# Gate blocks moved from the prompt's attention to the sample's attention, and a compression bias made once per cache, in a hybrid decoder step

## The chip, the cores and the metric

The kernel runs on one core of one Trainium2 chip. The metric is the time of one execution in microseconds (us) of device time; lower is better. Times of before are three runs, and one further execution was recorded by the profiler.

## What is computed

One layer of a hybrid trunk on 1024 prompt positions and 8 x 4 sample positions (1056 columns together, 1024 features). Two mixers run on the same normalised input: a gated MLP (mixer A), and sparse attention with a compressed, a selected and a window branch (mixer B). Their outputs pass through sigmoid gates and an output projection, and an MLP follows. In the reference's words:

```
x = x + (sigmoid(g_a) * (o_a @ w_branch[:A]) + sigmoid(g_b) * (o_b @ w_branch[A:])) @ w_out
h = rms_norm(x, g_norm2)
return x + square(relu(h @ w_up)) @ w_down
```

The compression that feeds the compressed branch is, per cache (keys, values):

```
bias = pe.reshape(-1) @ w1
return gelu(first[:, :-1] + second[:, 1:] + bias) @ w2
```

It is done once for the prompt's own rows and once for each of the sample's 8 caches of 2048 positions. `pe` and `w1` are the same for both, so `bias` is the same as well. For the sample, the selected branch reads 13 of 32 key blocks; the kernel reads all of them and masks.

## The kernel before, in words

Weight matrices are cut into 128-column blocks, 102 in all. Of these, block numbers 0 to 15 of a set that the code calls FM_MG give the merge gates (tanh of half the sum, stored to `th_d`), and 16 to 19 give mixer A's `u` (gelu, multiplied with the stored `s_d`, stored to `o_d`). "Gate block" stands for any of these 20 below. A gate block is worked in three column chunks of 352 columns; one chunk is 24 matmuls into one bank `G`, since each 32-bit operand is split into a high and a low part and three products are summed over 8 k-tiles. Weight blocks pass through a class `Weights`: a load (tile `wraw`), a high part on ACT and a low part by a subtraction on GpSimd (tile `whl`), one block ahead.

The stages, in program order:

1. Projections of keys, values, queries, and mixer A's `v`.
2. The prompt's attention: 32 pairs (8 query blocks of 128, 4 head pairs). For pair u, `a_steps` makes logits in bank `S` (three buffers), maxima on DVE, exponentials on ACT, a scale on GpSimd; `c_steps` transposes the probabilities (bank `PT`, `T`), splits them into two parts (tile `PH`, ACT then DVE) and multiplies with V in bank `O` (`PV`); `E` stores the result (tile `o_o`). Query block 7 has 27 key blocks to a pair.
3. The compression of the sample's caches (`c_weights`, 16 units, bank `F`); it is emitted after the attention, and is scheduled into it.
4. The sample's attention: two groups G of four sequences, each with five chunks c (four of selected keys, one of the window): ten chunks in all. One chunk is 2 MB in one of two `ring` buffers (NRB = 2): 16 page loads on SP, of 128 KB, or four loads of 512 KB for the window. A chunk is logits (`s_logits`, four matmuls j, one for each sequence, each needs its own four page loads), a masked maximum on DVE, an exponential on ACT, four transposes, and `values` (16 matmuls into `O`), which is the last reader of the ring buffer. Then `fin_group`.
5. What is left of the gate blocks, then the branch projection (`half_block`: tiles `OA`, from mixer B's output, and `OU`, from mixer A's), output projection and MLP to the end.

Tiles are assigned to engines by hand, but the order within an engine is set by a scheduler that follows data dependences and priority; earlier code has the higher priority. SP's order is kept as written in stages 3 and 4. So a gate block that is written late (line 1240 in before) may stand much earlier, where the scheduler saw room for it. It needs only the input `X`, a weight tile and bank `G`. The weight tiles of `W0` (pool `wst0`) are free from the start of the prompt's attention; those of `W1` (pool `wst`) lie where the attention's keys and values were (pool `kvp`) and so wait for its end.

NF0 says how many gate blocks belong to `W0` and NF1 is a second such number; before has 17 and 0. `OA` lies where the sample's ring was, and `OU` where `X` was, so neither can be filled before the sample's last `values` and the last gate block, respectively. Both are read back from `o_d` through four `ol` buffers.

Of the kernel before, what the change touches and what calls it, by code (L numbers as in the profile page):

```python
# [15 lines left out]
TB = 352  # L16
# [8 lines left out]
FM_KC, FM_VC, FM_MG, FM_U, FM_BR, FM_OUT, FM_MLP = 0, 1, 2, 18, 22, 30, 38  # L25
RAWA = 2
NRB = 2
DB = ("G", 1), ("F", 1), ("O", 1), ("PT", 2), ("PT", 2), ("S", 3), ("S", 3), ("S", 3)
NF0, NF1 = 17, 0
SB, FB = 3, 1  # L30
XRB = 4
QB = ("G", 1), ("F", 1)
# [13 lines left out]
def build(tc, a):  # L46
# [12 lines left out]
    def add(out, x, y):  # L59
        return tt(out, x, y, OP.add)  # L60
# [82 lines left out]
    knt = const("knt", [128, 2, 32])  # L143
    vn = const("vn", [32, 2, 128])
    expo = const("expo", [128, 16])
    onesf = const("onesf", [128, 2])

    X = big.tile([128, 2, 8, NT], F32R, name="big1")
    KT = kvp.tile([128, 4, NP], F32R, name="KT")
# [10 lines left out]
    def powcol(out, in_, n):  # L160
        POOL.tensor_tensor(out, in_, expo[:, 0:n], op=OP.pow)

    POOL.memset(onesf, 1.0)
    DVE.memset(f(ones), 1.0)
    cp(expo, f(ones)[:, 0:16], scale=-0.5)

# [259 lines left out]
        SP.dma_start(pe, a["pe" + "kv"[which]])  # L426
        return w1, pe, comp_w2(which, pl)

    def comp_bias(w1, pe, ps, pl):
        for o in range(8):  # L430
            mm(ps, w1[:, o], pe[:, o], o == 0, o == 7)
        tb = small([64, 2], "tb", 2, p=pl)
        cp(tb[:, 0:1], ps[64:128, 1:2])
        add(tb[:, 1:2], ps[0:64, 0:1], tb[:, 0:1])
        return tb[:, 1:2]

    def comp_hidden(ps, nch, bias, pl):

# [43 lines left out]
    def compress_prompt(which):  # L482
        w1, pe, w2 = comp_consts(which, pc)
        c2 = craw[which]
        pb = bank("F", 1) if which == 0 else bank("PT", 2)
        for o in range(8):
            mm(pb[:, 0:128], w1[:, o], c2[:, :, o], o == 0, o == 7)
        pbb = bank("G", 1) if which == 0 else bank("PT", 2)
        bias = comp_bias(w1, pe, pbb[:, 0:2], pc)
        g = comp_hidden(pb[:, 0:128].rearrange("p (k c) -> p k c", k=2), 64, bias, pc)  # L490
        DVE.tensor_copy(g[:, 64:128], g[:, 0:64])
        pb2 = bank("G", 1) if which == 0 else bank("O", 1)
        comp_out(pb2[:, 0:128], g, w2)
        if which == 0:
            z = comp_knorm(pb2[:, 0:128], pc, gkc, 2)
            ks = small([128, 2, 2, 64], "ckx", 1, F32R, p=pc)
            z3 = z.rearrange("p (h d) -> p h d", d=64)
            DVE.tensor_copy(ks[:, :, 0], z3)
            sub(ks[:, :, 1], z3, f(ks[:, :, 0]))
            pt = bank("F", 1)  # L500
            for kv in range(2):
                PE.transpose(pt[:, kv * 128:(kv + 1) * 128], f(ks[:, kv].rearrange("p a d -> p (a d)")), ident)
            cp(KTC, pt[:, 0:256].rearrange("p (k c) -> p k c", k=2)[:, :, 0:64])
        else:
            z3 = pb2[:, 0:128].rearrange("p (h d) -> p h d", d=64)
            POOL.memset(f(V2C), 0.0)
            for h in range(2):
                r = slice(64 * h, 64 * h + 64)
                cp(V2C[r, h, :, 0], z3[r])
                sub(V2C[r, h, :, 1], z3[r], f(V2C[r, h, :, 0]))  # L510
# [440 lines left out]
    def c_weights(which):  # L951
        w1r = pa.tile([128, 8, 128], F32, name="w1r", tag="hl", bufs=HIB)
        ACT.dma_start(w1r, a["w1" + "kv"[which]])
        w1 = pa.tile([128, 2, 8, 128], F32R, name="w1s", bufs=1)
        split(w1[:, 0], w1[:, 1], w1r)
        pe = small([128, 8, 2], "pes", 1, p=pa)
        ACT.dma_start(pe, a["pe" + "kv"[which]])
        w2 = comp_w2(which, pa)
        pb = bank("F", FB, psS)
        return w1, comp_bias(w1r, pe, pb[:, 0:2], pa), w2  # L960

    cl = Ahead([lambda w=w, b=b: c_load(w, b) for w in range(2) for b in range(8)], RAWA)
    ctxm = tc.manual_schedule(engines={mybir.EngineType.SP})
# [44 lines left out]
    def fillers(W, blocks, tag):  # L1008
        n = 0
        for b in blocks:  # L1010
# [12 lines left out]
                    evac(b, c, cs, ps)  # L1023
            W.ahead()

    def gate_evac3(b, c, cs, ps):
        zt = wst0.tile([128, TB], F32, name="zt", bufs=2) if b < NF0 else fp.tile([128, TB], F32, name="yt", bufs=2)
        mul(zt, ps[:, 0:TB], rep[:, cs])
        ACT.activation(zt, zt, AF.Tanh, scale=0.5)
        (ACT if b < 8 else POOL).dma_start(th_d[b, :, cs], zt)  # L1030
# [12 lines left out]
        POOL.dma_start(o_d[b - 16, :, cs], y)  # L1043

    W0 = Weights(wst0, 1, range(FM_MG, FM_MG + NF0))
    ps3 = pool("ps3")
    p3 = pool("p3")
    regs.clear()
# [99 lines left out]
        DVE.tensor_reduce(nm[:, 5:7], pn, axis=AX.X, op=OP.max, negate=True)  # L1148
        news.append((pn, nm))
    hp.__exit__(None, None, None)  # L1150
    fillers(W1, range(NF0, NF0 + NF1), lambda i: "S")

    def values(oc, c, blocks):

# [37 lines left out]
    for G in range(2):  # L1192
        pn, nm = news[G]
        sm = small([128, 8], "s_sm", 2, p=p3)
        oc = p3.tile([128, 6, 128], F32, name="oc", bufs=2)
        pt = bank("PT", 2, psS)
        PE.transpose(pt[:, 0:128], pcs[G], ident)
        ph = p3.tile([128, 5, 128], F32, name="s_ph", bufs=2)
        cp(ph[:, 0], pt[:, 0:128])
        values(oc, 5, [(ph[:, 0], vct[:, 4 * G:4 * G + 4])])  # L1200
        for c in range(5):
            br = c // 4
            kv = kvl()
            S = bank("S", SB, psS)
            s_logits(S, qp, G, lambda j: kv[:, :, j, 0:128])
            P = p3.tile([128, 512], F32, name="s_P", bufs=3)
            if c < 4:
                DVE.tensor_tensor_reduce(P.rearrange("p (b k) -> p b k", k=64), S.rearrange("p (b k) -> p b k", k=64),
                                         smask[:, G, c * 8:(c + 1) * 8, None].to_broadcast([128, 8, 64]),
                                         scale=-1.0, scalar=3e38, op0=OP.add, op1=OP.min, accum_out=nm[:, c:c + 1])  # L1210
            else:
                add(S[:, 0:4], S[:, 0:4], mwc)
                DVE.tensor_reduce(nm[:, c:c + 1], S, axis=AX.X, op=OP.max, negate=True)
            if c % 4 == 0:
                tt(nm[:, c:c + 1], nm[:, c:c + 1], nm[:, 5 + br:6 + br], OP.min)
                ACT.activation(pn[:, br], pn[:, br], AF.Exp, bias=nm[:, c:c + 1], accum_out=sm[:, 5 + br:6 + br])
            ACT.activation(P, P if c < 4 else S, AF.Exp, bias=nm[:, c:c + 1], scale=-1.0 if c < 4 else 1.0,
                           accum_out=sm[:, c:c + 1])
            ph = p3.tile([128, 5, 128], F32, name="s_ph", bufs=2)
            if c % 4 == 0:  # L1220
                pt = bank("F", FB, psS)
                PE.transpose(pt[0:32, 0:128], pn[:, br], ident)
                cp(ph[0:32, 4], pt[0:32, 0:128])
            pt = bank("PT", 2, psS).rearrange("p (a t) -> p a t", t=128)
            for e in range(4):
                PE.transpose(pt[:, e], P[:, e * 128:(e + 1) * 128], ident)
            cp(ph[:, 0:4], pt)
            blocks = [(ph[:, e], kv[:, e, :, 128:256]) for e in range(4)]
            if c % 4 == 0:
                blocks.append((ph[0:32, 4], vn[:, br]))  # L1230
            values(oc, c, blocks)
            if c == 1 and done:
                fin_group(*done)
        done = G, nm, sm, oc
# [2 lines left out]
    p3.release()  # L1237
    ps3.release()

    fillers(W0, range(NF0), lambda i: "G")  # L1240
    fillers(W1, range(NF0 + NF1, 20), lambda i: "GF"[i % 2])
    fp.release()
    wst0.release()

# [293 lines left out]
```

## Time and profile of before

| | us |
|---|---|
| median of 3 runs | 1848.17 |
| lowest and highest | 1847.6, 1854.99 |
| the profiled execution, device time | 1848.68 |
| its span, first to last instruction | 1846.9 |
| TensorE busy | 1761.8 (95%) |
| DVE, ACT, GpSimd busy | 949.0, 703.1, 414.0 |
| mean granted TensorE clock | 0.982 |

Busy time of an engine is the time in which it had at least one instruction in work; matmuls overlap, so a listed duration is longer than the distance between starts. The granted clock is 1.00 at TensorE's upper level (2.4 GHz) and 0.50 at its lower one (1.2 GHz); a value in between is a stretch with both. All positions are in us from the span's start.

### The profile page before, as it was taken

To read this page: it belongs to the slowest core of one execution; us is meant where nothing else is said; L and a number is where in the kernel's file an instruction comes from. 1 tells how busy PE (TensorE), PEld (TensorE's weight loads), DVE (VectorE), ACT (ScalarE), POOL (GpSimd) and SP (SyncE) were. 2 spreads that over 40 slices of the span, in tenths; PEclk is the share of its full clock that TensorE was granted. 3 is DMA by queue.
4 is the path that set the end of the run, shared out by engine and by line. 5 is a ranking of instruction groups with operands and counts; after the bars stand their busy time and mean duration, and the time that the engine had idled before them with its cause. 6 is when DMAs were issued, how large, how long until landed. Compare 5 with 4: busy or idle time off the path is not lost.

```text
span 1846.9 us, 30397 instructions
## 1 busy us (share of the span) xinstructions
PE 1761.8 (95%) x11127; PEld 1659.8 (90%) x11127; DVE 949.0 (51%) x2373; ACT 703.1 (38%) x1683; POOL 414.0 (22%) x604
## 2 busy tenths in 40 slices
PE   8999989999899999876999999999999999999999
PEld 6877889999899998523999999999999999999999
DVE  7637878777767777211765445333333333333332
ACT  5534577767667765211422332200330033003300
POOL 3103456555556655200200220000000000000000
PEclk9999989999999999987999999999999999999999
DMA  5332454333323313664553221111111111111121
GB/s 198 95 95 64 142 151 124 93 95 89 98 68 98 96 63 121 205 189 149 183 161 121 92 77 46 46 46 46 46 46 46 46 47 46 46 46 46 45 78 64
DMA packets 157992, 168.75 MB, mean 91 GB/s; under 512 B 52113, under 2 KB 132626, under 8 KB 157842
## 3 DMA queue, kind: packets, MB, share of 16 engines
q1 hardware_dynamic: 140194, 135.77, 23.9%
q0 software_dynamic: 6464, 20.19, 3.3%
q10 hardware_dynamic: 11184, 10.83, 1.8%
q8 instruction: 88, 1.44, 0.3%
q14 instruction: 62, 0.51, 0.1%
HBM read 136.56 MB, written 29.13 MB: 90 GB/s over the span
## 4 chain that ended last, share of the span: by engine, by line
PE 80%; DVE 5%; SPq 5%; DMA 3%; ACT 3%; issue 2%; POOL 1%; ACTq 0%; DVEq 0%; POOLq 0%; another core or an unknown queue 0%
PE S L73 26%; PE G L73 16%; PE PT L73 14%; PE F L73 10%; PE O L73 10%; SPq L932 3%; PE PT L844 3%; SPq L924 2%; DMA ol<-o_d 1%; ACT P L783 1%; PE PT L699 1%; DVE S L774 1%; DMA xr<-xT 0%; DVE PH L57 0%; ACT PH L54 0%
## 5 line engine op out<-in xcount | busy, mean ns | idle before, releaser
L54 ACT ACTIVATE whl<-wraw 128x1024 fp32r<-128x1024 f32 x100 | 106.1, 1061 | 411.2 <-PE S L73 144.2
L73 PE MATMUL G<-big,whl 128*128 128x352 f32 x1344 | 255.2, 333 | 2.5 <-ACT whl L54 1.5
L73 PEld LDWEIGHTS G<-big,whl 128*128 128x128 f32 x1344 | 220.6, 193 | 13.4 <-issue 5.0
L73 PE MATMUL S<-U,whl 128*128 128x352 f32 x864 | 201.6, 324 | 0.0
L73 PE MATMUL S<-H,whl 128*128 128x352 f32 x840 | 190.4, 324 | 0.0
L73 PE MATMUL PT<-U,whl 128*128 128x352 f32 x576 | 154.9, 324 | 0.0
L73 PEld LDWEIGHTS S<-U,whl 128*128 128x128 f32 x864 | 150.0, 188 | 0.0
L798 POOL TENSOR_SCALAR P<-P,rs 128x128 f32<-128x128 f32 (+4 forms) x272 | 132.8, 504 | 63.7 <-DVE rs L57 43.0
L73 PEld LDWEIGHTS S<-H,whl 128*128 128x128 f32 x840 | 144.9, 188 | 0.0
L73 PE MATMUL PT<-H,whl 128*128 128x352 f32 x528 | 143.2, 324 | 0.0
L783 ACT ACTIVATE P<-S,nm 128x512 f32<-128x512 f32 (+3 forms) x208 | 109.0, 532 | 44.1 <-DVE nm L57 32.9
L73 PE MATMUL S<-wt,big 128*128 128x512 f32 x408 | 104.1, 402 | 10.0 <-ACT wt L54 6.5
L57 DVE TENSOR_TENSOR PH<-PT,PH 128x512 fp32r<-128x512 f32 (+2 forms) x160 | 98.2, 618 | 29.6 <-ACT PH L54 28.1
L118 DVE TENSOR_TENSOR whl<-wraw,whl 128x1024 fp32r<-128x1024 f32 x80 | 97.7, 1222 | 14.6 <-ACT whl L54 14.6
L73 PEld LDWEIGHTS PT<-U,whl 128*128 128x128 f32 x576 | 103.3, 188 | 0.0
L73 PE MATMUL F<-H,whl 128*128 128x352 f32 x312 | 101.1, 324 | 0.0
L73 PE MATMUL O<-PH,V 128*128 128x256 f32 x528 | 92.1, 296 | 9.4 <-DVE PH L57 9.0
L73 PEld LDWEIGHTS S<-wt,big 128*128 128x128 f32 x408 | 76.1, 191 | 27.2 <-ACT wt L54 6.5
L54 ACT ACTIVATE PH<-PT 128x512 fp32r<-128x512 f32 (+2 forms) x160 | 86.1, 545 | 36.2 <-PE PT L844 35.3
L73 PE MATMUL O<-H,whl 128*128 128x352 f32 x312 | 99.0, 324 | 0.0
L73 PE MATMUL S<-KT,QT 128*128 128x128 f32 (+3 forms) x416 | 95.5, 340 | 2.9 <-ACT P L783 2.1
L73 PE MATMUL G<-H,whl 128*128 128x352 f32 x312 | 97.5, 324 | 0.5 <-DVE r L1373 0.5
(376 smaller groups left out, 3821.2 us busy)
## 6 DMA issues: line engine op xcount, KB each, us to landing
wraw<-wfm SPq DMA_DIRECT2D x80, 512.0 KB, 3.2
ring<-cs SPq DMA_DIRECT2D x128, 128.0 KB, 2.4
wraw<-wfm POOLq DMA_DIRECT2D x20, 512.0 KB, 3.9
tg<-th_d SPq DMA_DIRECT2D x48, 176.0 KB, 2.9
qdl<-qd_d SPq DMA_DIRECT2D x64, 128.0 KB, 2.5
raw<-cck SPq DMA_DIRECT2D x128, 64.0 KB, 1.8
raw<-ccv SPq DMA_DIRECT2D x128, 64.0 KB, 1.8
wtr<-wtok SPq DMA_DIRECT2D x24, 256.0 KB, 2.7
```

Source lines behind the costliest of these rows:

```text
L54: return ACT.activation(out, in_, AF.Copy, scale=scale)
L57: return DVE.tensor_tensor(out, x, y, op=op)
L73: return PE.matmul(out, l, r, start=start, stop=stop, skip_group_check=skip)
L118: (POOL if i < FM_BR else DVE).tensor_tensor(t[:, 1], raw, f(t[:, 0]), op=OP.subtract)
L699: PE.transpose(pt[:, j], src[:, j], ident)
L774: DVE.tensor_tensor_reduce(S, S, m, scale=-1.0, scalar=3e38, op0=OP.add, op1=OP.min, accum_out=dst)
L783: ACT.activation(Ps[c][:, lo:hi], Ss[c][:, lo:hi], AF.Exp, bias=nm[:, 0, k:k + 1], scale=todo[h, br, i], accum_out=sm[:, i, k:k + 1])
L798: POOL.tensor_scalar(P, P, rs[:, 1, k:k + 1], 1.0, op0=OP.mult, op1=OP.mult)
L844: PE.transpose(pt[:, j], Ps[c][:, j * 128:(j + 1) * 128], ident)
L924: _, vals = nc.values_load_multi_w_load_instructions(ptab[0:1, i0:i0 + 16], engines=[mybir.EngineType.SP], min_val=0, max_val=159, skip_ru ...
L932: SP.dma_start(dst, src)
```

## The change

NF0 becomes 12 and NF1 becomes 2. `W0`'s 12 blocks are still written so that the scheduler may place them anywhere from the start of the prompt's attention on; they are now written ahead of the sample's attention instead of behind it. The other eight (block numbers 12 to 19, `W1`) go through a generator, `fill`, which yields after each column chunk; the sample's loop takes two of them (NF1) right behind each chunk's logits, so 20 of the 24 column chunks stand in the loop, and the remaining four are taken behind it. All use bank `G`; before, the last three blocks alternated between `G` and `F`. The compression's bias is kept in a constant tile `cbias` when the prompt's compression makes it, and `c_weights` no longer loads `pe` or makes it again.

```diff
-NF0, NF1 = 17, 0
+NF0, NF1 = 12, 2
...
-    def comp_bias(w1, pe, ps, pl):
+    def comp_bias(which, w1, pe, ps, pl):
...
-        add(tb[:, 1:2], ps[0:64, 0:1], tb[:, 0:1])
-        return tb[:, 1:2]
+        add(cbias[:, which:which + 1], ps[0:64, 0:1], tb[:, 0:1])
+        return cbias[:, which:which + 1]
...
-        pe = small([128, 8, 2], "pes", 1, p=pa)
-        ACT.dma_start(pe, a["pe" + "kv"[which]])
         w2 = comp_w2(which, pa)
-        pb = bank("F", FB, psS)
-        return w1, comp_bias(w1r, pe, pb[:, 0:2], pa), w2
+        return w1, cbias[:, which:which + 1], w2
...
+    def fill(W, blocks, tag):
+        for b in blocks:
+            w = W.get(FM_MG + b)
+            for c in range(3):
+                cs = slice(c * TB, (c + 1) * TB)
+                ps = bank(tag, 1, psS)
+                for k in range(8):
+                    mm(ps[:, 0:TB], w[:, 0, k], X[:, 0, k, cs], k == 0, False)
+                    mm(ps[:, 0:TB], w[:, 0, k], X[:, 1, k, cs], False, False)
+                    mm(ps[:, 0:TB], w[:, 1, k], X[:, 0, k, cs], False, k == 7)
+                with tc.high_priority():
+                    (gate_evac3 if b < 16 else u_evac)(b, c, cs, ps)
+                if c == 2:
+                    W.ahead()
+                yield
...
     W0 = Weights(wst0, 1, range(FM_MG, FM_MG + NF0))
+    fillers(W0, range(NF0), lambda i: "G")
...
-    fillers(W1, range(NF0, NF0 + NF1), lambda i: "S")
+    f1 = fill(W1, range(NF0, 20), "G")
...
             s_logits(S, qp, G, lambda j: kv[:, :, j, 0:128])
+            for _ in range(NF1):
+                next(f1, None)
...
-    fillers(W0, range(NF0), lambda i: "G")
-    fillers(W1, range(NF0 + NF1, 20), lambda i: "GF"[i % 2])
+    for _ in f1:
+        pass
```

Three places show how the order on TensorE moves. The first is the end of the prompt's attention (`O_67..<-PH` is the last pair's `PV`, `V2C` its last operand; `G_` with `whl` is a gate chunk). Before:

```order
L73 MATMUL G_11856<-big1_77,whl_11851 128x352 x22
L73 MATMUL O_6768<-PH_6825,V2_80 128x256 x2
L73 MATMUL O_6768<-PH_6825,V2C_81 128x256 x2
L73 MATMUL G_11885<-big1_77,whl_11851 128x352 x24
L73 MATMUL G_11914<-big1_77,whl_11851 128x352 x24
```

Now:

```order
L843 MATMUL PT_6820<-ident_68,P_6710 128x128 x3
L73 MATMUL O_6767<-PH_6813,V2_80 128x256 x4
L1211 MATMUL PT_9911<-ident_68,pcs_9795 128x128
L73 MATMUL O_6767<-PH_6824,V2_80 128x256 x2
L73 MATMUL O_6767<-PH_6824,V2C_81 128x256 x2
L73 MATMUL G_10229<-big1_77,whl_10226 128x352 x2
L73 MATMUL F_9896<-knt_73,qp_9866 32x32 x8
```

Before, gate chunks run through to the end of the attention, and 1104 of the 1440 gate matmuls stand ahead of its last matmul. Now 864 do (all of `W0`), the last of them just behind the queries' transposes (`PT` with `qdl`) for pair 28 (numbered from 0), and G_10229 behind the last `V2C` is the first of `W1`. Ahead of the same transposes stand 794 gate matmuls before and 856 now.

The second place is the middle of the sample's loop on TensorE (`S_..<-ring` logits, one row per sequence unless it says x2 or x3; `PT_..<-s_P` the transposes; `O_..<-ring` values). Before, from the third chunk's end:

```order
L73 MATMUL S_9514<-ring_9183,qp_8791 32x512
L73 MATMUL S_9552<-ring_9365,qp_8791 32x512
L1226 MATMUL PT_9523<-ident_68,s_P_9519 128x128 x4
L73 MATMUL O_9529<-ring_9183,s_ph_9522 32x128 x16
L73 MATMUL S_9552<-ring_9365,qp_8791 32x512 x3
L73 MATMUL S_9734<-ring_9547,qp_8791 32x512
```

Now, from the same chunk's end:

```order
L73 MATMUL S_10717<-ring_10321,qp_9866 32x512
L73 MATMUL G_10823<-big1_77,whl_10780 128x352 x24
L73 MATMUL S_10818<-ring_10568,qp_9866 32x512
L1242 MATMUL PT_10789<-ident_68,s_P_10785 128x128 x4
L73 MATMUL S_10818<-ring_10568,qp_9866 32x512
L73 MATMUL G_10852<-big1_77,whl_10780 128x352 x23
L73 MATMUL O_10795<-ring_10321,s_ph_10788 32x128 x16
L73 MATMUL S_10818<-ring_10568,qp_9866 32x512
L73 MATMUL G_10852<-big1_77,whl_10780 128x352
L73 MATMUL S_10818<-ring_10568,qp_9866 32x512
```

Between a chunk's last logits and its values stand now, beside its transposes, two sequences' logits of the next chunk and 47 gate matmuls; before, it was one sequence's logits and no gate matmul.

The third place is the end of the loop. Before:

```order
L1226 MATMUL PT_10416<-ident_68,s_P_10406 128x128 x4
L73 MATMUL F_12095<-big1_77,whl_12056 128x352 x24
L73 MATMUL O_10422<-ring_10363,s_ph_10412 32x128 x16
L73 MATMUL O_10422<-vn_74,s_ph_10412 128x128
L73 MATMUL F_12174<-big1_77,whl_12169 128x352 x24
L73 MATMUL G_12210<-big1_77,whl_12169 128x352 x4
```

Now:

```order
L73 MATMUL G_12258<-big1_77,whl_12253 128x352 x23
L73 MATMUL O_12170<-ring_11962,s_ph_12160 32x128 x16
L73 MATMUL O_12170<-vn_74,s_ph_12160 128x128
L73 MATMUL G_12258<-big1_77,whl_12253 128x352
L73 MATMUL G_12294<-big1_77,whl_12253 128x352 x20
L1195 MATMUL PT_12203<-ident_68,oc_11162 128x128
L73 MATMUL G_12294<-big1_77,whl_12253 128x352 x4
L73 MATMUL F_12492<-oa_12380,whl_12366 128x352
L73 MATMUL G_12330<-big1_77,whl_12253 128x352 x24
```

Behind the last values stood six gate chunks; now there are two and one matmul.

## Rows read from the trace of the kernel before

**Rows 1.** Busy time by windows: stretch, length, PE, PEld, DVE, ACT, POOL, clock, DMA, GB/s

```profile
276.00:322.00 46.00, 43.55 (x327) 42.68 (x325) 39.52 (x141) 35.68 (x115) 32.34 (x57) 1.00 0.44 122
...
611.00:736.30 125.30, 120.99 (x890) 116.04 (x888) 94.31 (x270) 79.72 (x229) 74.63 (x119) 1.00 0.30 90
...
879.30:926.60 47.30, 44.83 (x270) 43.31 (x270) 33.38 (x72) 20.97 (x46) 9.72 (x15) 1.00 0.60 189
926.60:1846.90 920.30, 915.68 (x5642) 915.09 (x5642) 354.56 (x611) 194.22 (x344) 22.95 (x21) 1.00 0.19 62
```

**Rows 2.** The same for TensorE's matmuls with tile whl alone, 611 to 736

```profile
611.00:736.30 125.30, 58.00 (x311) 1.00 0.30 90
```

**Rows 3.** TensorE in order of time, attention's end: start, length, instructions

```profile
735.74 0.40 PE L73 MATMUL O<-PH,V2C 128*128 128x256 f32 x2
```

**Rows 4.** SP's issues in order of time, 740 to 860

```profile
740.81 5.53 SPq L932 DMA_DIRECT2D ring<-cs  x8
...
808.41 50.11 SPq L932 DMA_DIRECT2D ring<-cs  x64
```

**Rows 5.** TensorE's waits, 737 to 872: total us, times, longest

```profile
PE S L73 <- DMA ring<-cs: 24.0, 17, 3.1
```

**Rows 6.** Waits of SP's queue, 690 to 930

```profile
SPq L932 <- PE O L73: 10.5, 2, 5.6
```

**Rows 7.** Passage to the dense part, in order of time, TensorE, DVE and ACT

```profile
878.76 0.48 PE L73 MATMUL O<-vn,s_ph 32*128 32x128 f32 x2
...
898.62 0.49 DVE L57 TENSOR_TENSOR oa<-ol,oa 128x320 fp32r<-128x320 f32 x1
...
907.22 1.64 ACT L54 ACTIVATE ou<-ol 128x352 fp32r<-128x352 f32 x4
...
920.02 0.50 ACT L54 ACTIVATE ou<-ol 128x352 fp32r<-128x352 f32 x1 [0.98 <-DMA ol<-o_d]
...
929.89 0.33 PE L73 MATMUL PT<-oa,whl 128*128 128x352 f32 x1
```

**Rows 8.** TensorE in order of time: pair 28's query transposes, two gate chunks

```profile
611.09 0.60 PE L699 MATMUL PT<-ident,qdl 128*128 128x128 f32 x4
...
891.04 4.05 PE L73 MATMUL G<-big,whl 128*128 128x352 f32 x24
894.94 4.04 PE L73 MATMUL F<-big,whl 128*128 128x352 f32 x24
```

**Rows 9.** DVE's gate evacuations (598 to 672); GpSimd and DVE around 535

```profile
L57 DVE TENSOR_TENSOR zt<-G,rep 128x352 f32<-128x352 f32 x6 | 3.1, 520 | 3.6 <-PE G L73 3.6
...
535.00 2.34 POOL L118 TENSOR_TENSOR whl<-wraw,whl 128x1024 fp32r<-128x1024 f32 x1
...
535.41 1.95 DVE L57 TENSOR_TENSOR nm<-nm 128x1 f32<-128x1 f32 x1
```

**Rows 10.** TensorE, the bias made for the sample's key cache

```profile
252.58 1.93 PE L73 MATMUL F<-pes,w1r 128*128 128x2 f32 x16
```

**Rows 11.** GpSimd's first subtraction after the attention; TensorE's pieces of the sample's attention

```profile
739.31 2.38 POOL L118 TENSOR_TENSOR whl<-wraw,whl 128x1024 fp32r<-128x1024 f32 x1 [0.24 <-POOL o_o L873]
...
757.75 1.05 PE L73 MATMUL S<-ring,qp 128*32 128x512 f32 x4
759.19 1.02 PE L73 MATMUL S<-ring,qp 128*32 128x512 f32 x2 [0.39 <-DMA ring<-cs]
...
765.36 0.60 PE L1226 MATMUL PT<-ident,s_P 128*128 128x128 f32 x4
...
778.81 1.08 PE L73 MATMUL O<-ring,s_ph 128*32 128x128 f32 x32
```

**Rows 12.** Landing of the transfers into ol, from the tile's view

```profile
DMA to landing us min/median/max: 2.8/3.7/4.6
```

**Rows 13.** TensorE by windows of 4 us: busy, clock, DMA, GB/s

```profile
496.00:500.00 4.00, 0.48 (x2) 1.00 0.43 127
500.00:504.00 4.00, 3.74 (x15) 0.57 0.37 131
```

More of the change, by code (lines that the diff above doesn't have):

```diff
@@ L145, in build @@
     expo = const("expo", [128, 16])
-    onesf = const("onesf", [128, 2])
+    cbias = const("cbias", [64, 2])
     X = big.tile([128, 2, 8, NT], F32R, name="big1")
@@ L161, in powcol @@
         POOL.tensor_tensor(out, in_, expo[:, 0:n], op=OP.pow)
-    POOL.memset(onesf, 1.0)
     DVE.memset(f(ones), 1.0)
@@ L488, in compress_prompt @@
         pbb = bank("G", 1) if which == 0 else bank("PT", 2)
-        bias = comp_bias(w1, pe, pbb[:, 0:2], pc)
+        bias = comp_bias(which, w1, pe, pbb[:, 0:2], pc)
         g = comp_hidden(pb[:, 0:128].rearrange("p (k c) -> p k c", k=2), 64, bias, pc)
```

## The prediction

> **What bounds the kernel now.** I read the busy times by windows first, then the waits of each engine, then the order in time of SP and TensorE. From 926.6 us to the end TensorE is busy 915.7 of 920.3 us [rows 1]; the change touches nothing there, so that part keeps its length and only its start can move. What is in play is 611 to 930 us. In it lie three stretches with three different limits.
>
> The end of the prompt's attention, 611.0 to 736.3: TensorE is busy 121.0 of 125.3 us, DVE 94.3 [rows 1]. That looks like a TensorE bound, but 58.0 of the 121 us are 311 gate matmuls [rows 2], which go wherever the scheduler saw room, so the true limit without them may be DVE. I call the attention's end E; the last matmul on V ends at 736.14 [rows 3], and E is 736.3, where the next gate chunk starts.
>
> The sample's attention: SP issues the first page load at 740.81, and the last 64 from 808.41 to 858.52 [rows 4]. TensorE waited 24.0 us for page loads [rows 5], SP 10.5 us for a ring buffer [rows 6]. So SP paces it: 64 loads in 50.11 us, or 12.5 us for a chunk of 16. The reader is to see that TensorE has room here, and room alone.
>
> The passage to the dense part: the last values end at 879.24; OA's last split ends at 899.1, OU's splits on ACT run from 907.2 to 920.5, and the first two blocks' 144 branch matmuls are done at 929.9, where the third block's begin [rows 7]. TensorE is busy 44.8 of 47.3 us there [rows 1], because six gate chunks cover the reading back of OA.
>
> **The attention's end.** After the change 864 gate matmuls stand ahead of E in place of 1104. The stretch that starts with the transposes at 611.09 [rows 8] had 311 of them; now it has 8. But 856 instead of 794 stand ahead of those transposes.
> - Two gate chunks start 3.90 us apart [rows 8], so a gate matmul takes 0.1625 us. The 62 earlier ones cost 10.1 us if TensorE has no room for them, 0 if they fill holes; I take 8, since TensorE is nearly full there.
> - DVE's share: 13 evacuations at 0.52 us leave (6.8 us) [rows 9]. A low-part subtraction on GpSimd also holds DVE up: one of 2.34 us from 535.00 to 537.34 stands beside a DVE operation on a single column that lasted from 535.41 to 537.36, 1.95 us [rows 9]. Four blocks fewer in this stretch (311 matmuls are 4.3 blocks of 72) can give back up to 4 x 1.8, some 7 us, where each meets such an operation, and 0 where none does; I take 4. The Trainium skill, SBUF — State Buffer, section "Who interferes with whom", says that a DVE operation with two SBUF inputs and a GpSimd operation that reads SBUF exclude each other for a whole instruction; the row agrees. By that rule, taken for every block, it would be the 7, and the time some 4 us less than my sum.
> - That leaves 94.3 - 6.8 - 4 = 83.5 us of DVE work. At its present share (75%) the stretch takes 111 us; at the 86% that DVE reaches from 276 to 322 [rows 1] it takes 97. Bounds: 97, and 121 if nothing but the evacuations' 4 us or so is won. I take the middle of the two DVE shares, 104, so 21 us less; it is nearest to both rows.
> - The compression's bias: 16 records in 1.93 us at its first making [rows 10], and a second like it at 517, with four small instructions and two small loads. 0 to 4 us; I take 2. Nobody waits longer for the bias, since it exists long before.
>
> Sum: +8 - 21 - 2 = **15 us earlier**. The ends are 32 earlier (0 - 28 - 4) and 4 earlier: if gate matmuls fill nothing but holes, the 62 cost nothing either.
>
> **The sample's attention.** Positions are from E. Before, TensorE had gate chunks with ready weights at E. Now all blocks left are of `W1`, whose tiles wait for the attention's keys and values. The first low part after E ended at 741.69 [rows 11], so the first gate chunk starts at E+5.5 and TensorE is idle till then. TensorE's work up to the last values, from the new order, at the upper clock:
> - 22 gate chunks at 3.90: 85.8.
> - 40 logits: one alone takes 1.02, two side by side 1.05 [rows 11] (two records are one instruction). Nine pairs stand side by side: 22 x 1.02 + 9 x 1.05 = 32.
> - 10 x 0.60 transposes, 10 x 1.08 values [rows 11], with four extra small ones: 19; other small ones 2.
>
> That is 139. Waits on top: the second sequence's loads at the start, 3; ring buffers that come free late, 5 (a chunk's work is now 13.9 of TensorE against 12.5 of SP, so they meet almost evenly); bank G alone, four places where gate chunks follow each other directly, 0.65 each, 3; the first chunk at the lower clock after the idle time, 3. So the last values end at E + 5.5 + 139 + 14 = E+158.5; before it was 879.24 - 736.3 = E+142.9. **15.6 us later** counted from E. Bounds: 2 (no waits at all) and, with the slot wait below, 40.
>
> What hides behind what: SP's loads go on while TensorE works; SP waits for values, behind which nothing but its own loads is queued. GpSimd's queue holds, in order, weight loads, subtractions and the stores of gates; a store waits for its tanh, and the next subtraction behind it has a full block (11.7 us) of room.
>
> **The passage.** Counted from the last values, OA is ready 19.9 us later [rows 7]. It is a chain of loads through four buffers, which the change leaves alone. Before, OU then had to wait for the last gate chunk. Now only two chunks follow the values, so X is free after about 12 us, and OU's loads follow OA's: 19.9 + 3.7 (one load [rows 12]) + 0.5, then 13.3 from its first split to its last [rows 7], then about 2 of matmuls: 39.5. Before it was 929.9 - 879.24 = 50.7. **11 us earlier**, between 14 and 6. The cover is thinner, though: two gate chunks and 144 branch matmuls are 31 us of work, so TensorE idles some 8 us here. That is why four chunks less, 15.6 us, bring only 11.
>
> **Sum.** -15 + 15.6 - 11 = -10.4 us. Against the profiled execution's 1848.7 that is 1838.3; the median of the runs is 0.5 lower, so I forecast **1838**. The measurement can tell about 0.5%, or 9.2 us, from no change; the forecast stands at that edge.
>
> **Rivals.**
> 1. *Attention shrinks fully.* DVE runs at 86% or more and the earlier gate matmuls fill holes: E comes 30 us earlier. For it: DVE's present wait is mostly for a TensorE that is 97% busy. Against: the attention is a chain over four engines in fixed orders. 1848.7 - 30 + 15.6 - 11, about 1823.
> 2. *Gate matmuls only filled holes.* Then the attention doesn't get shorter by taking them out, E is 4 us earlier, for the evacuations and the bias. For it: they are the last in priority. Against: a 97% busy TensorE. 1849: no change.
> 3. *The ring buffer, slower.* A chunk's values now stand behind 47 gate matmuls and two of the next chunk's logits, and only they free the buffer for the chunk after next. It decides where the values end more than 12.5 us after SP began the next chunk's loads: SP stands still from then on. The second sequence's pages then land 8.5 us after the values (two groups of four issues at 3.1, and the landing), a third sequence's 11.6; 1 us of logits, 17 to 24 gate matmuls (up to 3.9) and 1.1 of values later the next buffer comes free. With two sequences ahead that is 14.5 us for a chunk, with three 17.6, against 14 in my sum. At 17.6 in eight chunks: +29, so 1867. For it: two such waits already [rows 6]. Against: in most chunks two sequences stand ahead, not three.
> 4. *The clock in the thinner attention.* In one slice TensorE was busy 0.48 of 4 us, and in the next the granted clock was 0.57 [rows 13]. Without gate matmuls, 121.0 - 58.0 + 8 x 0.1625, some 64 us, of TensorE work are left in 104 us. At 1.2 GHz throughout, that is 128 us: E comes at 611 + 8 + 128 - 2, 9 us later instead of 15 earlier, and the time would be 1862. The Trainium skill, TensorE: Matmul & The Clock Gate, Part 1, gives the rule that this hangs on: the throttled state is the default, and activity releases it. By the rows only short idle pieces brought the fall, and this stretch has work in every slice. I give it little.
>
> **How the numbers follow.** Forecast 0.42 (1838, own range 1830 to 1847); attention shrinks fully 0.20 (1823); holes 0.22 (1849); ring buffer 0.12 (1867); clock 0.04 (1862). Faster by over 0.5% (under 1839): a little over half of the forecast's case, 0.24, and the first rival, 0.20: 0.44. Slower by over 0.5% (above 1857.4): 0.12 + 0.04, and 0.02 of the holes' case: 0.18. Within: 0.38. The range goes from 1822 to 1860: it leaves out most of the two slow cases and the low end of the first rival.
>
> **What would show it.** E, the end of the last `V2C` matmul, near 721. No gate matmul with `whl` in the last 100 us ahead of it, and DVE's share there over 75%. The first page load 4.5 us after E; the last values near E+158, where before it was E+143. TensorE's granted clock near 1 in the sample's attention. The waits of S for page loads far under 24 us, SP's waits for values over 10.5. Idle TensorE after the last values for some 8 us. E later than 733 shows rival 2; SP waiting for values over 25 us shows rival 3; a clock under 0.8 in the last pairs rival 4. The prediction is wrong if the last values come much earlier than E+150 or the dense part starts other than some 40 us behind them.

## The result and the profile after

The changed kernel takes 1825.41 us (median of 4 runs, 1822.82 to 1826.23) against 1847.88 of the kernel before on the same chip (4 runs, 1847.21 to 1854.99): a ratio of 0.9867, with a 95% interval of 0.9841 to 0.9894, so 22.5 us faster. The forecast was 1838, half of that gain; the range (1822 to 1860) holds the result at its low end. The profiled execution has a span of 1822.9 us against 1846.9, 24.0 less.

Busy time by windows of the changed kernel, with the columns of [rows 1]: the end of the prompt's attention, the sample's attention, the passage, the dense part.

```profile
609.90:704.20 94.30, 76.03 (x540) 66.83 (x538) 77.60 (x248) 65.10 (x197) 48.02 (x88) 0.93 0.20 56
...
704.20:865.60 161.40, 147.89 (x1014) 107.87 (x1014) 45.49 (x115) 41.15 (x92) 39.97 (x47) 0.97 0.64 200
...
865.60:905.90 40.30, 35.18 (x197) 33.06 (x197) 26.59 (x60) 16.82 (x37) 2.16 (x4) 0.96 0.57 174
...
905.90:1822.90 917.00, 912.20 (x5622) 911.62 (x5620) 350.25 (x603) 193.48 (x343) 22.95 (x21) 1.00 0.18 61
```

In the stretch of the first row, TensorE waits above all for DVE's low parts of the probabilities (`PH`; total us, times, longest):

```profile
PE O L73 <- DVE PH L57: 9.1, 9, 2.7
PE F L73 <- DMA kct<-c_d: 2.3, 1, 2.3
PE F L73 <- DVE pcs L1126: 1.7, 1, 1.7
```

The dense part is as long as before (917.0 us; before it ran from 929.9 to 1846.9). The first row answers to the second of [rows 1]: the stretch from pair 28's transposes to E has shrunk from 125.3 to 94.3 us, and TensorE is no longer full in it (76.03 of 94.3). DVE's work in it fell from 94.31 to 77.60.

TensorE in order of time (start, length, instructions, and in brackets the idle time before a row and what ended it): pair 28's transposes, E, the first gate chunks of `W1`, the last values.

```profile
609.88 0.60 PE L698 MATMUL PT<-ident,qdl 128*128 128x128 f32 x4
...
703.78 0.40 PE L73 MATMUL O<-PH,V2C 128*128 128x256 f32 x2
...
707.24 0.95 PE L73 MATMUL G<-big,whl 128*128 128x352 f32 x2 [3.06 <-ACT whl L54]
709.72 2.71 PE L73 MATMUL G<-big,whl 128*128 128x352 f32 x8 [1.16 <-POOL whl L118]
...
864.15 1.08 PE L73 MATMUL O<-ring,s_ph 128*32 128x128 f32 x32
865.16 0.48 PE L73 MATMUL O<-vn,s_ph 32*128 32x128 f32 x2
```

The transposes come 1.2 us earlier than in [rows 8]. E is 704.2, and 736.3 before [rows 3]: 32.1 us earlier. The last values end at 865.6, or E+161.4, where it was E+142.9: 18.5 later from E. The dense part starts at 905.9, 40.3 after the values, where it was 50.7: 10.4 less. Sum: -32.1 + 18.5 - 10.4 = -24.0, all of the difference of the spans.

SP's issues in order of time, which answer to [rows 4]:

```profile
708.36 54.64 SPq L931 DMA_DIRECT2D ring<-cs  x64
767.03 2.67 SPq L1109 DMA_DIRECT2D ring<-cw  x4
780.35 45.02 SPq L931 DMA_DIRECT2D ring<-cs  x52
827.10 8.60 SPq L931 DMA_DIRECT2D ring<-cs  x12
```

The waits of SP's queue from 706 to 866 (total, times, longest), which answer to [rows 6]:

```profile
SPq L931 <- PE O L73: 15.8, 3, 9.3
...
SPq L1109 <- PE O L73: 9.0, 2, 5.1
```

TensorE's waits from E to the last values, which answer to [rows 5] (`zu` and `yt` are the evacuations of a gate chunk, which free bank `G`):

```profile
PE S L73 <- DMA ring<-cs: 6.1, 4, 2.5
...
PE G L73 <- DVE zu L57: 2.0, 4, 0.6
...
PE G L73 <- DVE yt L57: 0.9, 2, 0.7
```

SP now waits 24.8 us for values, while TensorE's waits for pages have gone from 24.0 [rows 5] to 6.1 us. TensorE, busy 147.89 of 161.4 us, paces the sample's attention, and SP waits for it.

### The profile page after: what moved, and what is told of

Same layout as the page of the kernel before. It is cut to its first block, busy times and chain, and to the rows that moved or that the text cites. A ratio compares the mean times of both kernels' runs of the same rounds, so it can differ in the third digit from the quotient of the medians.

```text
span 1822.9 us, 30327 instructions
## 1 busy us (share of the span) xinstructions
PE 1754.0 (96%) x11095; PEld 1655.3 (91%) x11095; DVE 939.5 (52%) x2371; ACT 701.7 (38%) x1681; POOL 411.3 (23%) x603
## 4 chain that ended last, share of the span: by engine, by line
PE 83%; DVE 7%; SPq 3%; DMA 2%; ACT 2%; issue 2%; POOL 1%; ACTq 0%; DVEq 0%; POOLq 0%
PE S L73 27%; PE G L73 18%; PE PT L73 14%; PE F L73 10%; PE O L73 10%; PE PT L843 2%; SPq L931 2%; DVE PH L57 1%; SPq L923 1%; DMA ol<-o_d 1%; DMA ring<-cs 1%; DVE S L773 1%; PE PT L698 1%; ACT P L782 0%; DMA xr<-xT 0%
## 5 line engine op out<-in xcount | busy, mean ns | idle before, releaser
L73 PE MATMUL G<-big,whl 128*128 128x352 f32 x1440 | 271.1, 333 | 14.6 <-ACT whl L54 7.0
L73 PEld LDWEIGHTS G<-big,whl 128*128 128x128 f32 x1440 | 235.5, 191 | 43.4 <-issue 16.5
L797 POOL TENSOR_SCALAR P<-P,rs 128x128 f32<-128x128 f32 (+4 forms) x272 | 132.1, 501 | 77.6 <-DVE rs L57 51.0
```

Source lines behind the costliest of these rows:

```text
L73: return PE.matmul(out, l, r, start=start, stop=stop, skip_group_check=skip)
L797: POOL.tensor_scalar(P, P, rs[:, 1, k:k + 1], 1.0, op0=OP.mult, op1=OP.mult)
```

## The experiments

E, the last values (counted from E), the passage (from the values to the dense part, whose start is taken as the span less 917.0) and the span come from one profiled execution each; the median from the timed runs. e_again is the changed kernel a second time; its positions repeat within about 1 us. Not all do: e_nobias, whose order is that of before up to pair 30, reached pair 28 at 614.1 instead of 611.1, so 3 us at E is the finest that these single profiles tell. The profiled execution of e_w1s took 1836.56, 3 us less than its median.

| kernel | E | values after E | passage | span | median |
|---|---|---|---|---|---|
| before | 736.3 | 142.9 | 50.7 | 1846.9 | 1847.9 |
| changed | 704.2 | 161.4 | 40.3 | 1822.9 | 1825.4 |
| e_again | 703.2 | 162.5 | 40.6 | 1823.3 | 1824.9 |
| e_bias | 737.6 | 136.4 | 56.7 | 1847.7 | 1849.8 |
| e_nobias | 710.6 | 161.3 | 40.7 | 1829.6 | 1831.7 |
| e_dummy | 703.5 | 166.9 | 40.6 | 1828.0 | 1829.9 |
| e_w1s | 714.2 | 162.6 | 41.0 | 1834.8 | 1840.0 |
| e_nf10 | 689.7 | 160.8 | 71.6 | 1839.1 | 1839.2 |
| e_nf11 | 698.2 | 163.3 | 53.6 | 1832.1 | 1834.7 |
| e_nf13 | 717.4 | 159.8 | 35.8 | 1830.0 | 1831.2 |
| e_nf14 | 724.3 | 152.4 | 35.6 | 1829.3 | 1831.7 |
| e_gf | 705.1 | 161.5 | 41.1 | 1824.7 | 1823.9 |

### Each half of the change alone

The change has two parts, and in TensorE's order each can be seen apart. The bias edit alone moves 62 gate matmuls and 44 of the compression's matmuls (`F` from `hl` and `w1s`) ahead of pair 28's transposes; up to there, 12, 14 or 17 blocks give the same order. The prediction had counted the 62, but not the 44. e_bias is the kernel before with the bias edit:

```diff
...
-        return w1, comp_bias(w1r, pe, pb[:, 0:2], pa), w2
+        return w1, cbias[:, which:which + 1], w2
```

> The kernel before with the bias edit alone (17 blocks in the attention, as before). In TensorE's order it moves 62 gate matmuls and 44 of the compression's matmuls ahead of the transposes of pair 28, and leaves 24 gate matmuls of the 17 blocks behind E instead of 120. Theory A, the prediction's: the edit is worth its own small instructions, 2 us, and the order does not matter: E at 734, time 1845 to 1848. Theory B: the order matters, since 44 matmuls of 0.28 us (12.4 us) leave the last four pairs, and what comes ahead of them fills holes: E at 725 to 730, last values at E+135 to E+143, time 1828 to 1836.

Measured: 1849.77, ratio to before 1.001 (1.0001 to 1.002), E 737.6. Of theory B only the values came (E+136.4), not its E and not its time; A's time nearly did: alone the edit brings nothing. 96 gate matmuls fewer stand behind E; the values come 6.5 us nearer to it, and the passage takes 6.0 back. Six gate chunks stand behind the values as before.

e_nobias undoes the same lines in the changed kernel.

> The changed kernel with the bias edit undone (12 blocks and the sample's chunks kept). TensorE's order is that of the kernel before up to pair 30, then without gate matmuls. Theory A: E within 4 us of the changed kernel's 704, time 1826 to 1830. Theory B: 52 matmuls of the compression more stand in the last four pairs, with their splits on ACT and GpSimd: E at 715 to 724, sample and passage as in the changed kernel, time 1836 to 1846.

Measured: 1831.7 (0.9914 of before, 0.9898 to 0.9931), E 710.6. This is between the theories, in B's direction, and 3 of the 6 us at E may be the spread named above. So the 12 blocks alone bring 16 us, and the bias edit 6 more on top of them, though it brought nothing alone.

Where do these 6 us come from? Two differences stand out in the traces. First a stall that [rows 13] had shown without its cause. In the kernel before, TensorE stood still before 500.26; DVE and GpSimd in order of time show why:

```profile
495.38 1.22 DVE L57 TENSOR_TENSOR w1s<-w1r,w1s 128x1024 fp32r<-128x1024 f32 x1
496.51 2.43 DVE L448 SCALAR_TENSOR_TENSOR ch_y<-ch_y,ch_x 128x128 f32<-128x128 f32 x1
...
495.92 2.87 POOL L118 TENSOR_TENSOR whl<-wraw,whl 128x1024 fp32r<-128x1024 f32 x1 [4.13 <-ACT whl L54]
...
500.26 1.15 PE L73 MATMUL O<-PH,V 128*128 128x256 f32 x4 [3.78 <-DVE PH L57]
```

`PH` waits on DVE behind the low part of the second cache's weights (`w1s`) and a `ch_y` held up by GpSimd's subtraction (2.43 us). In the changed kernel `w1s` comes at 474.64 instead of 495.38, and the same three pairs have no stall:

```profile
474.64 1.23 DVE L57 TENSOR_TENSOR w1s<-w1r,w1s 128x1024 fp32r<-128x1024 f32 x1 [0.60 <-ACT w1s L54]
```

Busy time of these pairs by windows, before and changed:

```profile
489.40:552.50 63.10, 56.22 (x382) 54.70 (x381) 44.22 (x137) 40.48 (x115) 34.50 (x58) 0.92 0.29 87
```

```profile
488.80:543.60 54.80, 54.80 (x409) 54.08 (x408) 38.67 (x124) 39.39 (x114) 33.21 (x52) 1.00 0.37 106
```

The stall alone doesn't make the 6 us, though. From pair 19's transposes to pair 28's it takes 179.1 us in the kernel before and in e_nobias, and 178.6 in the changed kernel: what was won was filled with gate and compression matmuls that stood later.

Second, the compression's end. Tile views (minimum, median and maximum in ns, then first and last start) of the compression's matmuls and of the ranking that selects the sample's blocks; before, then changed, then e_dummy (below):

```profile
L73 PE MATMUL F<-hl,w1s x384: 272/281/367, 266.8 to 687.5; 128*128 128x256 f32 x192
L1132 DVE TENSOR_REDUCE cnt<-rkA x4: 604/616/624, 720.9 to 734.5; 128x15 f32<-128x450 f32 x4
```

```profile
L73 PE MATMUL F<-hl,w1s x384: 272/282/385, 264.8 to 646.5; 128*128 128x256 f32 x192
L1146 DVE TENSOR_REDUCE cnt<-rkA x4: 601/608/611, 681.1 to 695.0; 128x15 f32<-128x450 f32 x4
```

```profile
L73 PE MATMUL F<-hl,w1s x384: 272/282/370, 269.6 to 683.4; 128*128 128x256 f32 x192
L1151 DVE TENSOR_REDUCE cnt<-rkA x4: 607/616/622, 710.8 to 722.2; 128x15 f32<-128x450 f32 x4
```

In the changed kernel the compression is through 41 us earlier than before, and the ranking ends 9 us ahead of E. Not all of the 41 us are the bias edit's: with 17 blocks it brings the last of these matmuls from 687.5 to 661.1 (e_bias), with 12 from 682.6 (e_nobias) to 646.5.

e_dummy keeps the stored bias, but puts the instructions back:

```diff
         w2 = comp_w2(which, pa)
+        pe = small([128, 8, 2], "pes", 1, p=pa)
+        ACT.dma_start(pe, a["pe" + "kv"[which]])
+        pb = bank("F", FB, psS)
+        for o in range(8):
+            mm(pb[:, 0:2], w1r[:, o], pe[:, o], o == 0, o == 7)
```

> The changed kernel with the bias's load and its 16 matmuls per cache put back where they were, their result unused (the hidden layer takes the stored bias). TensorE's order is then the old one again (794 gate and 284 compression matmuls ahead of pair 28). Theory order: the stall of TensorE at 495 to 500 is back, E at 709 to 712, time 1830 to 1834. Theory dependence (the hidden layer's wait for the bias is what costs): E at 703 to 706, time 1824 to 1828.

Measured: 1829.88 against 1824.94 of e_again in the same set of runs. The time is all but the order theory's, and a stall is there; a window of 4 us of e_dummy:

```profile
500.00:504.00 4.00, 0.59 (x2) 0.30 (x2) 4.00 (x4) 2.34 (x6) 3.28 (x2) 1.00 0.47 141
```

But E is the other theory's, 703.5, by two differences that cancel: pair 19 comes 5.1 us later than in the changed kernel, pair 28 2.9 earlier. The 5 us lie behind E: the ranking ends at 722.8, and the small logits on the sample's new keys (`knt`) wait for `s_new`, which DVE makes between two steps of the ranking. DVE and TensorE in order of time in e_dummy:

```profile
720.64 0.62 DVE L57 TENSOR_TENSOR rkB<-rkB,tri 128x450 f32<-128x450 f32 x1
721.17 0.22 DVE L57 TENSOR_TENSOR s_new<-F,mnew 128x64 f32<-128x64 f32 x1
721.31 0.62 DVE L57 TENSOR_TENSOR rkA<-rkA,rkB 128x450 f32<-128x450 f32 x1
...
721.45 0.44 PE L73 MATMUL F<-knt,qp 128*32 128x32 f32 x16 [4.44 <-DVE s_new L57]
```

So the hidden layer's wait for the bias is not what costs: without it the time is that of e_nobias. With 12 blocks and the later compression the ranking is no longer done when the attention ends, but that its lateness is the price is not shown. In e_nobias, where it ends at 725.7, the same matmuls wait even longer, 7.17 us, and the values still come at E+161.3, as in the changed kernel. What e_nobias loses, it has lost by E: it is 4.2 us later at pair 28 (614.1 against 609.9), and from there to E takes 96.4 us instead of 94.3. Of the 4.2, 3 are also lost to the kernel before, in the same order, between the transposes of pair 4 and of pair 5. A wait of TensorE in e_nobias there, and the window of 250 to 262 us in e_nobias and then in before:

```profile
PE F L73 <- DMA pes<-pek: 1.7, 1, 1.7
```

```profile
250.00:262.00 12.00, 10.26 (x55) 10.11 (x55) 6.79 (x26) 8.18 (x24) 6.13 (x10) 0.69 0.70 202
```

```profile
250.00:262.00 12.00, 12.00 (x79) 11.92 (x77) 7.65 (x27) 8.12 (x25) 7.29 (x12) 0.81 0.82 236
```

TensorE waited there for the load of `pe`, which the edit takes out, and its granted clock was 0.69 over these 12 us; in before, where it did not wait for `pe`, it was 0.81. Whether that load comes late in most executions, single profiles can't tell. So the 6 us stand in the times, but their cause stays open. Why the edit brings nothing with 17 blocks is argued only: the ranking of before ends at 735.1, still ahead of its later E, and 120 gate matmuls of `W0` stand behind E to run meanwhile.

e_w1s makes the bias per cache from the two split halves, so that the raw tile gives back its buffer (one of two that the compression's inputs share) after the split. Its edit against e_nobias:

```diff
...
-        return w1, comp_bias(w1r, pe, pb[:, 0:2], pa), w2
+        return w1, comp_bias([f(w1[:, 0]), f(w1[:, 1])], pe, pb[:, 0:2], pa), w2
```

> The changed kernel with the bias made per cache as before, but from the two split halves of the weights in place of the raw tile, so that the raw tile, which takes one of the two buffers of the compression's inputs, is free after the split. Theory buffer: the stall of TensorE at 495 to 500 (second cache's weights) goes and E is 704 to 707, time 1825 to 1828. Theory order only: E at 710, time 1831 to 1834, as with the old bias.

Measured: 1839.95 (1833.14 to 1842.22), E 714.2. Neither. `w1s` does come at 479.7 and the compression ends at 664, but pair 28 is reached at 619.3, 9 us late, with a stretch from 500 to 510 at a granted clock of 0.66. It is a third order, and a worse one. Why the scheduler deals the attention so differently for a few small instructions stays open.

### TensorE's work or the work beside it

A gate chunk costs TensorE 24 matmuls, and DVE, ACT and GpSimd its evacuation, tanh, weight split and subtraction. Two kernels take one side away for the last five of 17 blocks, on e_bias, whose order up to pair 28 is the changed kernel's. e_noside leaves out loads, splits and evacuations of these blocks (their gates are other data):

```diff
...
+            if W is W0 and b >= 12:
+                evac = lambda b, c, cs, ps: POOL.dma_start(th_d[b, :, cs] if b < 16 else o_d[0, :, cs], rep[:, cs])
...
-    W0 = Weights(wst0, 1, range(FM_MG, FM_MG + NF0))
+    W0 = Weights(wst0, 1, range(FM_MG, FM_MG + 12))
```

> The kernel with the bias edit alone, but the last five blocks of the attention (12 to 16) left without their side work: no weight load, split or subtraction, no evacuation and no tanh; their 336 matmuls stay and use block 11's weights, and their stores write other data (outputs of the gates are wrong). 361 gate matmuls then stand behind the transposes of pair 28. Theory TensorE: E depends on TensorE's work alone and stays at 733 to 738. Theory side work (DVE, ACT and GpSimd set the last pairs): E at 704 to 712. The prediction's own terms (DVE 10.8 us at 75 to 86%) give 724.

e_nomm keeps all that and leaves out 23 of the 24 matmuls:

```diff
-                for k in range(8):
+                if W is W0 and b >= 12:
+                    mm(ps[:, 0:TB], w[:, 0, 0], X[:, 0, 0, cs], True, True)
+                for k in range(0 if W is W0 and b >= 12 else 8):
```

> The kernel with the bias edit alone, but each chunk of blocks 12 to 16 ahead of the attention's end has 1 matmul instead of 24 (gates of these blocks are wrong); weight loads, splits, subtractions, evacuations and stores stay. 23 gate matmuls stand behind the transposes of pair 28. Theory TensorE: E at 704 to 709, as in the changed kernel. Theory side work: E at 728 to 738.

Each ran once (1839.48 and 1822.13 us). Busy time by windows from pair 28's transposes to E, in e_bias, e_noside and e_nomm:

```profile
610.40:737.60 127.20, 122.00 (x877) 117.45 (x875) 90.43 (x265) 77.58 (x216) 69.36 (x111) 0.99 0.24 73
```

```profile
612.80:735.80 123.00, 122.36 (x894) 118.83 (x893) 80.43 (x248) 66.25 (x197) 48.95 (x88) 1.00 0.16 43
```

```profile
609.60:717.40 107.80, 84.37 (x555) 72.94 (x553) 94.47 (x267) 76.59 (x220) 71.91 (x115) 0.90 0.33 99
```

e_noside has E at 735.8, as the TensorE theory has it: without the side work the stretch is only 4.2 us shorter (with 361 gate matmuls in it instead of 344), and TensorE is busy for 99% of it. e_nomm has E at 717.4, as no theory had it: without 321 matmuls (344 - 23; 52 us of TensorE's work at 0.1625) the stretch is 19.4 shorter, and DVE is now busy for 88%. With both gone, in the changed kernel, it is 32.9 shorter. So there are two limits, one behind the other: TensorE first, and 19 us below it another. That this is the chain through DVE is argued from DVE's 88%; TensorE's lower clock (0.90, in the changed kernel 0.93) may have a part in it, which no run measures by itself. The change lowers both limits.

What the side work costs DVE can be read from its groups of instructions in the same stretch, changed kernel first, then e_nomm:

```profile
L57 DVE TENSOR_TENSOR rs<-rs,sgate 128x2 f32<-128x2 f32 x15 | 4.2, 284 | 0.1
L57 DVE TENSOR_TENSOR nm<-nm 128x1 f32<-128x1 f32 x22 | 4.9, 224 | 0.1
L57 DVE TENSOR_TENSOR zt<-G,rep 128x352 f32<-128x352 f32 x1 | 0.5, 511 | 0.0
```

```profile
L57 DVE TENSOR_TENSOR rs<-rs,sgate 128x2 f32<-128x2 f32 x15 | 10.8, 721 | 0.2
L57 DVE TENSOR_TENSOR nm<-nm 128x1 f32<-128x1 f32 x22 | 6.3, 287 | 0.1
L57 DVE TENSOR_TENSOR zt<-G,rep 128x352 f32<-128x352 f32 x13 | 6.7, 513 | 0.4 <-PE G L73 0.4
```

12 more evacuations cost 6.2 us. The same 15 products `rs`, of two columns each, cost 6.6 more, `nm` 1.4, and three `ch_y` 1.8: 9.8 us in which DVE was held up beside five GpSimd subtractions of 2.35 to 2.37 us that the changed kernel does not have here, 2.0 for each. In order of time each of the five meets one such instruction: a `ch_y`, an `nm`, and three of the 15 `rs`, which lasted 2.08 to 3.32 us. The evacuation, which reads one operand from PSUM, takes the same 0.51 in both. This is the rule of the Trainium skill, SBUF — State Buffer, section "Who interferes with whom", that the prediction weighed; the traces agree with it.

### Other numbers of blocks, other banks

Four kernels have 10, 11, 13 and 14 blocks in the attention, by one edit, here for e_nf14:

```diff
-NF0, NF1 = 12, 2
+NF0, NF1 = 14, 2
```

> The changed kernel with 14 blocks in the attention and 6 for the sample (18 chunks). The last four pairs get 152 gate matmuls instead of 9. Theory full price (TensorE sets the last pairs): 143 x 0.1625 = 23 us, E at 727, time 1832. Theory holes (the four-engine chain sets them; TensorE idle 18.2 of 94.2 us takes the matmuls in): E at 705 to 711. Sample then paced by SP, values at E+147, passage 39: time 1810 to 1816.

> The changed kernel with 10 blocks in the attention and 10 for the sample (30 chunks, of which about 7 stand behind the last values). 136 gate matmuls leave pairs 26 to 28. Theory full price: E 22 us earlier, at 682; values at E+158; the passage grows to about 58: time 1817. Theory holes: E at 700 to 704, time 1835 to 1839.

> The changed kernel with 13 blocks in the attention and 7 for the sample (21 chunks, none behind the last values). Theory smooth (price of a gate matmul ahead of E 0.13 us, after E covered by the page loads or not, a parabola through the times at 10, 12 and 14): E at 714, time 1826, no difference from 12. Theory kink (the sample is still bound by TensorE at 13, so a block less there gives back 11.7 us, and costs 10 in the attention): time 1822 to 1824.

> The changed kernel with 11 blocks in the attention and 9 for the sample. By the parabola: E at 697, time 1830. Theory kink (from 12 downwards every further block stands behind the last values, at its full 11.7 us, against 7.3 us won ahead of E): 1829 to 1832, the values still at E+158 to E+161 and the passage some 12 us longer than the changed kernel's 40.

Measured: 1839.2, 1834.7, 1831.2 and 1831.7 at 10, 11, 13 and 14, and 1824.9 to 1825.4 at 12. For e_nf14 the full price came nearer (E 724.3, not 709), and the time was its 1832. For e_nf10 E was between the two, but the passage was 71.6 instead of 58, which gave the holes theory's time. e_nf13 was 5 us over the parabola: E at 717.4 instead of 714, and the values hardly nearer to it; the kink theory's 1822 to 1824 was further off. e_nf11 was near its forecast in E and values, with a passage 13 us longer, but its time lies 3 to 5 us above both theories. From 10 to 14 blocks E moves by 34.6 us, 8.7 a block or 0.12 us a gate matmul, of the 0.1625 that one takes. Below 12 each further block stands behind the last values and costs 13 to 18 us there; above 12 the sample gives back less than the attention takes (12 to 14: E +20.1, values and passage -13.7). 12 is the best of the five.

Taking NF1 from 2 to 0 leaves TensorE's order as it is, row for row; the scheduler puts the chunks in the same places without the pin. It was not timed. e_gf lets the sample's chunks alternate between two banks:

```diff
...
-    f1 = fill(W1, range(NF0, 20), "G")
+    f1 = fill(W1, range(NF0, 20), "GF")
```

> The changed kernel with the sample's gate chunks alternating between the banks G and F instead of G alone. The prediction's term for G alone was 3 us: values at E+158 instead of E+161.5, time 3 us less (1822). Rival: F is also the bank of the sample's small transposes and the gaps at G are filled by logits; no change, or chunks crowd ahead of the values (549 matmuls instead of 527 stand ahead of the last), E+164, and the passage gives 3 to 4 us back: time within 2 us of the changed kernel's.

Measured: 1823.93 (1820.96 to 1826.46), ratio to before 0.9874 (0.9852 to 0.9896): the changed kernel's time, within its spread, with the values at E+161.5. The rival's time held. The gaps at bank G are there, though: TensorE's waits for evacuations went from 2.9 us (2.0 + 0.9) to this one:

```profile
PE G L73 <- DVE yt L57: 0.7, 1, 0.7
```

The time so won went to gate matmuls: 550 instead of 528 stand ahead of the last values, which come no later for it. But the passage is no shorter with 22 fewer behind them (41.1 us), so closing the gaps brought nothing. No kernel tried that computes the same was clearly faster than the changed one.

## Why the prediction was half right

The sample and the passage came out near their terms; the attention's end did not. E was to come 15 us earlier and came 32 earlier. Of these 17 us, 7 stood ahead of pair 28's transposes and 10 behind them. The signs of being wrong were set at the values and the passage, where the prediction held, and not at an E that came too early.

- **What bounds it.** The three stretches, and which engine paces the sample, were right: the dense part kept its 917 us, and SP's waits for values and TensorE's for pages changed places.
- **The earlier gate matmuls, +8: this step failed.** Pair 28's transposes came at 609.9, 1.2 earlier than before, not 6 later (+8 - 2); in e_bias, with the same order up to there, at 610.4. 62 gate matmuls (10 us) and 44 of the compression's (5 us: two of them take 0.40 us where one takes 0.28, so each adds 0.12, and the expectation of e_bias took the listed 0.28) had gone in at no cost. Some half of the room for them is the stall at 495 to 500 in [rows 13] (three pairs in 54.8 us instead of 63.1); the rest was not traced to one place. The prediction read those rows for the clock and did not ask what had stopped TensorE, nor whether the bias edit moved it.
- **The stretch, -21: mis-sized, it measured -31.** 83.5 us of DVE's work were expected at a share of 80%, 77.6 came at 82% (of 94.3). The share is luck in part: e_nobias had 74.5 of 96.4 us (77%), e_nomm 94.47 of 107.8 (88%). The work was taken too high, and not for the subtractions. In the kernel before, three of the four held up a product `nm` (0.15 us where nothing holds it), together 4.5 us, near the 4 that was taken; DVE and GpSimd in order of time:

```profile
642.81 2.39 POOL L118 TENSOR_TENSOR whl<-wraw,whl 128x1024 fp32r<-128x1024 f32 x1 [0.74 <-ACT whl L54]
643.22 2.01 DVE L57 TENSOR_TENSOR nm<-nm 128x1 f32<-128x1 f32 x1
...
676.93 2.38 POOL L118 TENSOR_TENSOR whl<-wraw,whl 128x1024 fp32r<-128x1024 f32 x1
678.18 1.15 DVE L57 TENSOR_TENSOR nm<-nm 128x1 f32<-128x1 f32 x1
...
704.93 2.37 POOL L118 TENSOR_TENSOR whl<-wraw,whl 128x1024 fp32r<-128x1024 f32 x1 [3.83 <-ACT whl L54]
705.54 1.78 DVE L57 TENSOR_TENSOR nm<-nm 128x1 f32<-128x1 f32 x1
```

The evacuations gave 6.2 us, near the 6.8 that were taken for them. The other 6 us are in small parts that were put at nothing: among them the compression work that left the stretch (GpSimd's subtractions for `hl` in it went from 11 to 6, and they held DVE up too: a `ch_y` of 0.28 us took 1.31). That was in the order, but wasn't looked for there.
- **The bias, -2.** With 12 blocks it is worth 6 us, with 17 none, so it is not the time of its own instructions alone; the order of all the others changes with it, and what of that costs the 6 us stays open.
- **The sample, +15.6 from E; 18.5 measured.** The first gate chunk started at E+3.1 and its main part at E+5.5, as worked out. SP's waits, 24.8 us, stood just under the 25 at which rival 3 was to show, yet the values came 3 us late only, since TensorE had chunks to run meanwhile. The 3 us for bank G were there (2.9 us of waits), but e_gf shows that nothing is won by closing these gaps.
- **The passage, -11; -10.4 measured,** with 5.1 us of idle TensorE (40.30 - 35.18) where 8 were expected.
- **The rivals.** The first, at a chance of 0.20, gave 1823, and E 30 us earlier; 32 came. Its reason, DVE at 86% or more, was not the one; the earlier matmuls did fill holes, and DVE had less to do, so that its number came is luck in part. The second, that gate matmuls only filled holes, falls: they cost 0.12 us each near E. The clock was 0.93 in the stretch, so the fourth did not come.

## What to carry to other kernels

An engine that is 97% busy with filler is not shown to be the only limit: take the filler out and leave its side work in, then the reverse, and see where the next limit lies. Ahead of a forecast, compare the whole order of all the work that a scheduler places, not only that of the work being moved: here a small edit moved another stage's end by 26 to 36 us, and was worth 6 us beside the other edit and nothing without it. And where an idle piece stands in the trace, find what stopped the engine there and ask whether the change takes that away.

## What was not expected of the hardware

A product of two columns on DVE, 0.16 us where nothing holds it up, took 2.08 to 3.32 us three times in e_nomm, each started beside a GpSimd subtraction on a weight block of 2.35 to 2.37 us. So the 15 such products cost 6.6 us more than in the changed kernel (721 ns on average instead of 284), as much as 12 evacuations of 352 columns (6.2).
